# Expert layer: tokens fetched by indirect DMA a pair ahead, results added in place, weight rows dealt out in pairs, other places at the end

## The chip, the cores and the metric

One NeuronCore of a Trainium2 chip runs the whole program; seven cores are idle. The metric is the time of one execution on the device, in microseconds (us). Below, PE is the matrix engine (PEld its weight loads), DVE, ACT and POOL are the vector, scalar and GpSimd engines, and SP is the engine whose queue issues most of the DMAs.

## The reference

512 tokens of 1024 features go through two blocks. The first is a gated linear recurrence beside an attention, then a mixture of 16 experts in which each expert chooses its own 64 tokens; the second is another attention block with a feed-forward part, which the change does not touch. The expert layer, cut to what matters:

```
def expert_choice_moe(h, w_router, w_gate, w_up, w_down):
    cap = EC_CAPACITY_FACTOR * length // N_EXPERTS            # 64
    aff = softmax(h @ w_router)                               # [512, 16]
    gate, idx = lax.top_k(swapaxes(aff, 1, 2), cap)           # per expert
    xe = h[bidx, idx]
    hid = silu(einsum("becd,edf->becf", xe, w_gate)) * einsum("becd,edf->becf", xe, w_up)
    ye = einsum("becf,efd->becd", hid, w_down) * gate[..., None]
    return zeros_like(h).at[bidx, idx].add(ye)
...
x = x + g2 * expert_choice_moe(rms_norm(x, norm2_g) * (1 + sc2) + sh2, ...)
```

All is float32. Each expert has three 1024x1024 matrices, 12 MiB; the 16 experts have 192 MiB, or 201.3 MB, and every byte of it is read once.

## The kernel before, in words

**Stages.** `first_mixer` and the merge end in `mix_out` (L937), which multiplies by w_out, adds the product to `X` (the tokens, 128 partitions x 4 x 1024, in SBUF), transposes X (L955) and forms the router's logits. `router` (L982) takes the softmax, and in eight rounds of max and match_replace the 64 tokens of each expert; its result `sl` says for each token and expert which of the 64 slots it holds. `moe` (L1024) is the expert layer. Then come the second block's stages, from L1197 on.

**The loop over pairs.** `moe` takes two experts at a time, p = 0 to 7, with 64 slots each, so 128 columns. For a pair, `prep` (L1100 on) compares `sl` with a row of numbers to make a one-hot matrix D (L1089), scales it by each token's 1/rms, and gathers the tokens by 32 matmuls of X with D (L1105, 64 instructions on PE, as float32 goes through twice); DVE and ACT apply sc2 and sh2 on the way out of PSUM (L1107, L1110) into `xe`, which is already transposed. Then G = xe·w_gate and U = xe·w_up (both `gemm`, L1083, 32 matmuls of 64 slots x 512 each, 64 instructions), `back` (L1116: D once more, four transposes into `oh`, L1119, and the gate's values by four matmuls, L1124), `prep` of the next pair, hy = silu(G)·U (L1148), eight transposes (L1150), the down product Y (L1083). Y is split into a high and a low part in `yh` (L1173 to L1175), and 16 matmuls with `oh` (L1178, L1179) put each slot's result at its token; DVE adds them to `ACC` (L1181, L1184), two tiles of their own. In the last pair POOL adds ACC to X (L1171) and the products go straight into X. `ye` is the name for Y times gate and g2; the profile shows it as `hy`, as the buffer is shared.

**The order.** Each engine runs its instructions in the order in which a scheduler has put them, which stands before the run. It lets the scatter and the gather of the next pair run between the matmuls of a gemm.

**The weights.** Each weight load is 1 MiB: of 128x2x1024 (two rows of 4 KB per partition, 128 rows apart), issued by SP in the order of use. `mload` (L1035) deals out places for them in a fixed order, `kinds`: six "x1", three "raw", three "hl" (each two halves of 512 KB, L1052), three "x2", with four single places more and the two of ACC in the first round, 21 MiB in all, loaded before the layer starts. A load waits on SP until the matmuls on the former content of its place are done, and all loads behind it on SP wait with it. The last pair's down product goes by `gemm_parts` (L1062), in three parts of 512, 256 and 256 columns; its 12 loads (rows of 2 KB and 1 KB) use the three "x2" places and `rw2`, in turn, three times (L1046, L1059).

Of the kernel before, what the change touches and what calls it, by code (L numbers as in the profile page):

```python
# [20 lines left out]
def constants():  # L21
# [31 lines left out]
    iota = np.repeat(np.arange(1, 65, dtype=f)[None, :], 128, axis=0)  # L53
    return {
# [6 lines left out]
    }  # L61

# [6 lines left out]
class Build:  # L69
# [111 lines left out]
    def first_mixer(self):  # L181
# [19 lines left out]
        at = 0  # L201
# [12 lines left out]
        put("n2", I["norm2_g"][0].rearrange("(r p) -> r p", p=128), 8)  # L214
        put("lb", I["hg_lb_logits"].rearrange("a b (h p) -> (a b h) p", p=128), 16)
        put("hgn", I["hg_norm_g"][0].rearrange("(r p) -> r p", p=128), 4)
        self.prow = rows
# [9 lines left out]
        nc.vector.tensor_copy(self.pcol, tp[:, :128])  # L227
        cs = p1.tile([128, 8, 32], F32, name="cs")
# [157 lines left out]
        es1.close()  # L386
        esw = ExitStack()
# [20 lines left out]
    def ctx_part(self, cx, rest):  # L408
# [20 lines left out]
        def shift(i):  # L429
            for j, at in enumerate((0, 1, 2, 3)):  # L430
                if at == i:
                    self.mod_col(cx, pc, (self.sh2, self.sc2)[j // 2], 3 + j // 2, j % 2)
# [18 lines left out]
        nc.vector.scalar_tensor_tensor(self.sc2, self.sc2, 1.0, self.c("n2"), op0=ALU.add, op1=ALU.mult)  # L451
# [473 lines left out]
    def mod_col(self, pool, psp, out, wi, half, tag="mr"):  # L925

        nc = self.nc
        for s, row in self.mod_rows(pool, psp, wi, tag, (half,)):
# [4 lines left out]
            c = 8 * wi + 4 * s  # L933
            nc.vector.tensor_tensor(out[:, 4 * s:4 * s + 4], ps[:, :8].rearrange("p (k i) -> p k i", i=2)[:, :, 0],
                                    self.c("bmod")[:, c:c + 4], op=ALU.add)

    def mix_out(self, end):  # L937
# [3 lines left out]
        nc.sync.dma_start(wr, I["w_router"][0].rearrange("(k p) e -> p k e", p=128))  # L941
# [19 lines left out]
        for n, ks in enumerate(self.wN(I["w_out"][0], 0, 1024)):  # L961
            s = slice(n * 256, (n + 1) * 256)
            for b in range(4):
# [18 lines left out]
    def router(self):  # L982

        nc, mo, ms, pp = self.nc, self.mo, self.ms, self.pmx
        iota = self.iota = ms.tile([128, 64], F32, name="iota")
        nc.sync.dma_start(iota, self.I["k_iota"])
        rs = self.rs = ms.tile([128, 4], F32, name="rs")
# [3 lines left out]
        e = self.aff = ms.tile([128, 4, 16], F32, name="aff")  # L991
# [32 lines left out]
    def moe(self):  # L1024
# [4 lines left out]
        acc = [(self.mwx2, "acc0"), (self.mwx2, "acc1")]  # L1029
        kinds = ["x1"] * 6 + ["raw"] * self.nraw + ["hl"] * (self.nhl // 2) + ["x2"] * 3  # L1030
        self.tail = False
        todo = (kinds[:6] + [(self.rw1, "rw2"), (self.rw2, "rw")] + kinds[6:] +
                [(self.rw1, "rw"), (self.rw2, "rw2")] + acc)

        def mload(src, last):  # L1035
            if last == 2 and not self.tail:

                self.tail = True
                todo[:] = ["x2", "x2", "x2", (self.rw2, "rw2")] * 3
            if not todo:  # L1040
                todo.extend(k for k in kinds if not last or k != "hl")
            kind = todo.pop(0)
            shape = [128, src.shape[1], src.shape[2]]
# [10 lines left out]
            if kind == "raw":  # L1054
                t = self.wload(src, [128, 2, 1024])
            else:
                pool, n = (self.mwx, 6) if kind == "x1" else (ms, 3)
                t = pool.tile(shape, F32, name="mwt", tag="mwt", bufs=n)
                nc.sync.dma_start(t, src)  # L1059
            return [t[:, i] for i in range(shape[1])]  # L1060

        def gemm_parts(ps, lhs, wa, wb):  # L1062

            ws = [w.rearrange("(k p) f -> p k f", p=128) for w in (wa, wb)]
            for y, c in zip(ps, parts):
                for kk in range(2):
                    tl = [mload(w[:, 4 * kk:4 * kk + 4, c], 2) for w in ws]
# [19 lines left out]
        def onehot(p, tag, prev=None):  # L1087
            D = ms.tile([128, 4, 128], F32, name="D", tag=tag, bufs=1)
            ins = nc.vector.tensor_tensor(D.rearrange("p b (a s) -> p b a s", a=2),  # L1089
                                          self.iota.unsqueeze(1).unsqueeze(1).to_broadcast([128, 4, 2, 64]),  # L1090
                                          self.sl[:, :, 2 * p:2 * p + 2].unsqueeze(3).to_broadcast([128, 4, 2, 64]),
                                          op=ALU.is_equal)
            if prev:
                self.after(ins, prev)
            return D

        def prep(p):

            Ds = onehot(p, "Ds")
            nc.vector.tensor_tensor(Ds, Ds, self.rs.unsqueeze(2).to_broadcast([128, 4, 128]), op=ALU.mult)  # L1100
            xe = XE[p % 2]
            for k in range(8):
                ps = self.psmm()[:, :128]
                for b in range(4):
                    nc.tensor.matmul(ps, self.X[:, b, k * 128:(k + 1) * 128], Ds[:, b], start=(b == 0), stop=(b == 3))  # L1105
                if k % 2:
                    nc.scalar.activation(xe[:, k], ps, AF.Identity, bias=self.sh2[:, k:k + 1],  # L1107
                                         scale=self.sc2[:, k:k + 1])
                else:
                    ins = nc.vector.tensor_scalar(xe[:, k], ps, self.sc2[:, k:k + 1], self.sh2[:, k:k + 1],  # L1110
                                                  op0=ALU.mult, op1=ALU.add)
            return xe, ins

        def back(p, prev):

            D = onehot(p, "D", prev)  # L1116
# [3 lines left out]
            oh = ms.tile([128, 512], F32R, name="oh", tag="oh", bufs=1)  # L1120
            nc.scalar.activation(oh, ps, AF.Copy)
            gps = self.psmm()
            for b in range(4):
                nc.tensor.matmul(gps[:, :16], D[:, b], self.aff[:, b], start=(b == 0), stop=(b == 3))  # L1124
            gc = ms.tile([128, 1], F32, name="gc", tag="gc", bufs=2)
            for a in range(2):
                nc.vector.tensor_copy(gc[64 * a:64 * a + 64], gps[64 * a:64 * a + 64, 2 * p + a:2 * p + a + 1])
            return oh, gc
# [3 lines left out]
        xe, ins = prep(0)  # L1132
        for p in range(8):
# [11 lines left out]
            oh, gc = back(p, ins)  # L1145
            if p < 7:
                xe, ins = prep(p + 1)
            nc.vector.tensor_tensor(hs, hs, U, op=ALU.mult)  # L1148
            for k in range(8):
                nc.tensor.transpose(tp[:, k], hs[:, k * 128:(k + 1) * 128], self.ident)  # L1150
# [14 lines left out]
            yh = self.rw1.tile([128, 2, 1024], F32R, name="yh", tag="rw")  # L1165
            if p == 0:
                ACC = [pl.tile([128, 2, 1024], F32, name="acc", tag=t) for pl, t in acc]
                ACC = [ACC[b // 2][:, b % 2] for b in range(4)]
            elif p == 7:
                for b in range(4):  # L1170
                    nc.gpsimd.tensor_tensor(self.X[:, b], self.X[:, b], ACC[b], op=ALU.add)  # L1171
# [516 lines left out]
```

## Time and profile before

| | |
|---|---|
| median of 3 runs (lowest to highest) | 1816.25 us (1812.9 to 1819.8) |
| the profiled execution, its own time | 1816.96 us |
| its span in the trace | 1815.2 us |
| PE busy | 1710.9 us, 94% |
| DVE, ACT, POOL busy | 45%, 36%, 7% |
| moved by DMA | 327.73 MB, 181 GB/s over the span |
| first gate matmul of the expert layer | 641.7 us |
| first matmul of the second block (L1197) | 1142.8 us |
| chain that ended last | PE 63% of the span, DMA 1% |

The shares of the span are means over stages with different limits. The span is cut into 40 slices on the page, of 45.4 us each: the expert layer fills those from 642 to 1143 us, and from 726 to 1089 us, eight slices in a row, the DMA engines are nine tenths busy and more, which they are in hardly any other slice. PE's line shows nine tenths nearly everywhere. A PE row of the timeline is a run of instructions on one line that were not interrupted, its time in us, and in brackets how long PE stood idle before it and what ended that.

### The profile page before, as it was taken

To read this page: it belongs to the slowest core of one execution; us is meant where nothing else is said; L and a number is where in the kernel's file an instruction comes from. 1 tells how busy PE (TensorE), PEld (TensorE's weight loads), DVE (VectorE), ACT (ScalarE), POOL (GpSimd) and SP (SyncE) were. 2 spreads that over 40 slices of the span, in tenths; PEclk is the share of its full clock that TensorE was granted. 3 is DMA by queue.
4 is the path that set the end of the run, shared out by engine and by line. 5 is a ranking of instruction groups with operands and counts; after the bars stand their busy time and mean duration, and the time that the engine had idled before them with its cause. 6 is when DMAs were issued, how large, how long until landed. Compare 5 with 4: busy or idle time off the path is not lost.

```text
span 1815.2 us, 26611 instructions
## 1 busy us (share of the span) xinstructions
PE 1710.9 (94%) x11031; PEld 1247.3 (69%) x11031; DVE 824.7 (45%) x1605; ACT 655.2 (36%) x1137; POOL 131.9 (7%) x153
## 2 busy tenths in 40 slices
PE   5999899999999599999999998899999999999999
PEld 3987679666669553444434433697677989898989
DVE  5536885855343511221221221656675543434342
ACT  4638984656432210010000000655563242323131
POOL 0100000122110000000000010410221000000000
PEclk9999999999999799999999999999999999999999
DMA  9562122112458578999999996451002222323231
GB/s 308 184 206 76 48 71 65 60 37 92 168 174 298 210 304 317 409 409 384 393 375 362 407 383 229 131 163 50 22 24 70 83 91 84 115 72 116 71 115 48
DMA packets 177393, 327.73 MB, mean 181 GB/s; under 512 B 8580, under 2 KB 115816, under 8 KB 177272
## 3 DMA queue, kind: packets, MB, share of 16 engines
q1 hardware_dynamic: 176480, 325.44, 49.9%
q8 instruction: 87, 1.43, 0.3%
q10 hardware_dynamic: 744, 0.51, 0.1%
q14 instruction: 34, 0.28, 0.0%
q0 software_dynamic: 48, 0.08, 0.0%
HBM read 323.91 MB, written 2.10 MB: 180 GB/s over the span
## 4 chain that ended last, share of the span: by engine, by line
PE 63%; DVE 4%; DMA 1%; ACT 1%; issue 1%; POOL 0%; SPq 0%; DVEq 0%; ACTq 0%
PE mm L90 10%; PE mm L89 10%; PE mm L91 10%; PE G L1083 7%; PE U L1083 6%; PE Y L1083 5%; PE mm L1105 3%; PE po L1615 1%; PE mm L1178 1%; PE pt L1568 1%; PE mm L1179 1%; PE sc L1547 1%; DMA wraw<-in_w_in_dram 1%; PE sc L1548 1%; PE Y L1071 0%
## 5 line engine op out<-in xcount | busy, mean ns | idle before, releaser
L81 ACT ACTIVATE whi<-wraw 128x1024 fp32r<-128x1024 f32 (+1 forms) x171 | 173.4, 1018 | 365.0 <-PE mm L89 178.2
L83 DVE TENSOR_TENSOR wlo<-wraw,whi 128x1024 fp32r<-128x1024 f32 (+1 forms) x171 | 207.9, 1218 | 110.4 <-ACT whi L81 109.5
L90 PE MATMUL mm<-whi,ul 128*128 128x256 f32 x512 | 144.3, 282 | 0.0
L91 PE MATMUL mm<-whi,uh 128*128 128x256 f32 x512 | 143.2, 281 | 0.0
L89 PE MATMUL mm<-wlo,uh 128*128 128x256 f32 x512 | 143.1, 281 | 0.0
L90 PE MATMUL mm<-HXh,wlo 128*128 128x512 f32 x256 | 102.2, 399 | 1.8 <-DVE wlo L83 1.8
L89 PE MATMUL mm<-HXl,whi 128*128 128x512 f32 x256 | 103.5, 404 | 0.0
L91 PE MATMUL mm<-HXh,whi 128*128 128x512 f32 x256 | 101.2, 395 | 0.0
L89 PE MATMUL mm<-H,whi 128*128 128x512 f32 x256 | 99.7, 390 | 0.0
L91 PE MATMUL mm<-H,whi 128*128 128x512 f32 x256 | 99.6, 389 | 0.0
L90 PE MATMUL mm<-H,wlo 128*128 128x512 f32 x256 | 99.6, 389 | 0.0
L90 PEld LDWEIGHTS mm<-whi,ul 128*128 128x128 f32 x512 | 96.5, 188 | 1.0 <-DVE ul L1651 0.8
L89 PEld LDWEIGHTS mm<-wlo,uh 128*128 128x128 f32 x512 | 96.2, 188 | 0.2
L91 PEld LDWEIGHTS mm<-whi,uh 128*128 128x128 f32 x512 | 96.2, 188 | 0.0
L1105 PEld LDWEIGHTS mm<-D,X 128*128 128x128 f32 x512 | 61.9, 199 | 18.5 <-issue 15.4
L1660 DVE SCALAR_TENSOR_TENSOR X<-mm,r,X 128x256 f32<-128x256 f32 x64 | 30.9, 483 | 88.2 <-PE mm L91 88.2
L1105 PE MATMUL mm<-D,X 128*128 128x128 f32 x512 | 66.7, 288 | 2.8 <-DVE D L1100 1.8
L1148 DVE TENSOR_TENSOR hy<-hy,U 128x1024 f32<-128x1024 f32 x8 | 9.8, 1222 | 124.4 <-PE U L1083 124.4
L1083 PE MATMUL Y<-mwt,xh 128*64 128x512 f32 x240 | 59.9, 594 | 5.4 <-DVE xh L1151 5.4
L1646 DVE TENSOR_SCALAR r<-mm 128x512 f32<-128x512 f32 x32 | 22.1, 692 | 85.2 <-PE mm L91 85.2
L1173 DVE SCALAR_TENSOR_TENSOR hy<-Y,gc,g 128x512 f32<-128x512 f32 (+1 forms) x17 | 11.6, 715 | 106.4 <-PE Y L1083 100.2
L90 PEld LDWEIGHTS mm<-HXh,wlo 128*128 128x128 f32 x256 | 48.4, 189 | 13.8 <-DVE wlo L83 2.6
(539 smaller groups left out, 4073.0 us busy)
## 6 DMA issues: line engine op xcount, KB each, us to landing
mwt<-in_w_exp_gate_dram SPq DMA_DIRECT2D x41, 1024.0 KB, 9.1
mwt<-in_w_exp_up_dram SPq DMA_DIRECT2D x35, 1024.0 KB, 10.6
mwt<-in_w_exp_down_dram SPq DMA_DIRECT2D x33, 1024.0 KB, 13.2
wraw<-in_w_in_dram SPq DMA_DIRECT2D x29, 1024.0 KB, 5.1
wraw<-in_w_mod_dram SPq DMA_DIRECT2D x16, 1024.0 KB, 6.9
wraw<-in_w_up_dram SPq DMA_DIRECT2D x16, 1024.0 KB, 5.6
wraw<-in_w_down_dram SPq DMA_DIRECT2D x16, 1024.0 KB, 5.1
mwh<-in_w_exp_up_dram SPq DMA_DIRECT2D x30, 512.0 KB, 9.2
```

Of the source, the lines that this page charges most:

```text
L81: i1 = self.nc.scalar.activation(hi, src, AF.Copy)
L83: i2 = self.nc.vector.tensor_tensor(lo, src, hi, op=ALU.subtract)
L89: mm(ps, ah, bl, start=first, stop=False)
L90: mm(ps, al, bh, start=False, stop=False)
L91: mm(ps, ah, bh, start=False, stop=last)
L1083: nc.tensor.matmul(ps[64 * a:64 * a + 64, n], lhs[:, k, 64 * a:64 * a + 64], tl[a][k2][:, n * 512:(n + 1) * 512], start=(k == 0), stop=(k ...
L1105: nc.tensor.matmul(ps, self.X[:, b, k * 128:(k + 1) * 128], Ds[:, b], start=(b == 0), stop=(b == 3))
L1178: nc.tensor.matmul(ps, oh[:, b * 128:(b + 1) * 128], yh[:, 1, s], start=True, stop=False)
L1179: nc.tensor.matmul(ps, oh[:, b * 128:(b + 1) * 128], yh[:, 0, s], start=False, stop=True)
L1547: nc.tensor.matmul(sc, QS[:, h, s], KDl[:, br, p // 2, :n], start=True, stop=False)
L1646: nc.vector.tensor_scalar(r, ps, 0.0, None, op0=ALU.max)
L1660: nc.vector.scalar_tensor_tensor(self.X[:, b, s], ps, r2[:, b:b + 1], self.X[:, b, s], op0=ALU.mult, op1=ALU.add)
```

## The change

`mix_out` writes X to a DRAM copy `XD` (four DMAs from POOL's queue). A new function `chosen(p)` makes D and multiplies it by a table of 18 columns, which gives the gate, the token's number and its 1/rms for each slot; POOL then starts an indirect DMA that reads the 128 tokens' rows (4 KB each, 512 KB) from XD into `xg`. `prep` scales `xg` and transposes it (eight transposes). `chosen` of a pair is called a pair ahead. The scatter of two pairs (0 and 1, 2 and 3, 4 and 5) is summed in PSUM and added to X in place; pairs 6 and 7 go alone; ACC is gone. Weight rows 2p and 2p+1 of a block of 256 go to one partition, so that a partition's two rows are one piece of 8 KB in memory; every operand that meets them by its rows (`chunk(k)`: the transposes of X, xg and hy, sc2, sh2, the router's weights) is taken with a stride of two. The halves "hl" stay rows of 4 KB. Place "x3" is new and ACC's two places are gone, so 20 MiB are loaded before the layer starts. The last pair's 12 places are now x1, x1, rw2, x2, x2, x2, x1 (four times), rw2, x2.

```diff
+def chunk(k):
+    return slice(k // 2 * 256 + k % 2, k // 2 * 256 + 256, 2)
...
+        self.XD = dp.tile([512, 1024], F32, name="XD")
...
             for k in range(4):
-                nc.tensor.matmul(ps[:, 2 * k:2 * k + 2], row[:, k * 128:(k + 1) * 128], self.selc,
+                at = k // 2 * 256 + k % 2
+                nc.tensor.matmul(ps[:, 2 * k:2 * k + 2], row[:, at:at + 256 - k % 2:2], self.selc,
                                  start=True, stop=True)
...
-                    nc.tensor.transpose(tp[:, b * 128:(b + 1) * 128], self.X[:, b, k * 128:(k + 1) * 128], self.ident)
+                    nc.tensor.transpose(tp[:, b * 128:(b + 1) * 128], self.X[:, b, chunk(k)], self.ident)
...
+                if b == 3:
+                    nc.gpsimd.dma_start(self.XD.rearrange("(b p) f -> p b f", p=128)[:, :, s], self.X[:, :, s])
...
+        nc.gpsimd.tensor_copy(self.aff[:, :, 16], iota[:, 64:])
+        nc.gpsimd.tensor_copy(self.aff[:, :, 17], rs)
...
-        kinds = ["x1"] * 6 + ["raw"] * self.nraw + ["hl"] * (self.nhl // 2) + ["x2"] * 3
+        kinds = ["x1"] * 6 + ["raw"] * self.nraw + ["hl"] * (self.nhl // 2) + ["x2"] * 3 + ["x3"]
...
-                [(self.rw1, "rw"), (self.rw2, "rw2")] + acc)
+                [(self.rw1, "rw"), (self.rw2, "rw2")])
...
-                todo[:] = ["x2", "x2", "x2", (self.rw2, "rw2")] * 3
+                todo[:] = ["x1", "x1", (self.rw2, "rw2"), "x2", "x2", "x2", "x1", "x1", "x1", "x1",
+                           (self.rw2, "rw2"), "x2"]
...
-            wa = wa.rearrange("(k p) f -> p k f", p=128)
-            wb = wb.rearrange("(k p) f -> p k f", p=128)
+            ws = [w.rearrange("(k p j) f -> p k j f", p=128, j=2) for w in (wa, wb)]
             for kk in range(4):
-                tl = [mload(w[:, 2 * kk:2 * kk + 2, :], last) for w in (wa, wb)]
+                tl = [mload(w[:, kk], last) for w in ws]
...
+        def chosen(p):
+            if p > 7:
+                return None
+            xg = self.mwx2.tile([128, 1024], F32, name="xg", tag="xg", bufs=1)
+            D = onehot(p, "D")
+            ps = self.psmm()[:, :18]
+            for b in range(4):
+                nc.tensor.matmul(ps, D[:, b], self.aff[:, b], start=(b == 0), stop=(b == 3))
+            g = ms.tile([128, 18], F32, name="gs", tag="gs", bufs=3)
+            nc.vector.tensor_copy(g, ps)
+            at = ms.tile([128, 1], U32, name="at", tag="at", bufs=2)
+            nc.vector.tensor_copy(at, g[:, 16:17])
+            nc.gpsimd.indirect_dma_start(xg, None, self.XD, bass.IndirectOffsetOnAxis(ap=at, axis=0))
+            return xg, g
+        def prep(p, xg, g):
+            nc.vector.tensor_scalar(xg, xg, g[:, 17:18], None, op0=ALU.mult)
             xe = XE[p % 2]
-            for k in range(8):
-                ps = self.psmm()[:, :128]
-                for b in range(4):
-                    nc.tensor.matmul(ps, self.X[:, b, k * 128:(k + 1) * 128], Ds[:, b], start=(b == 0), stop=(b == 3))
...
+            for k0 in range(0, 8, 4):
+                ps = self.psmm()
+                for k in range(k0, k0 + 4):
+                    nc.tensor.transpose(ps[:, (k - k0) * 128:(k - k0 + 1) * 128], xg[:, chunk(k)], self.ident)
...
-            oh, gc = back(p, ins)
+            oh = back(p)
...
             if p < 7:
-                xe, ins = prep(p + 1)
+                xe = prep(p + 1, *ch)
+                gs, ch = ch[1], chosen(p + 2)
...
-            if p == 0:
-                ACC = [pl.tile([128, 2, 1024], F32, name="acc", tag=t) for pl, t in acc]
-                ACC = [ACC[b // 2][:, b % 2] for b in range(4)]
-            elif p == 7:
-                for b in range(4):
-                    nc.gpsimd.tensor_tensor(self.X[:, b], self.X[:, b], ACC[b], op=ALU.add)
+            yh = (ms if p % 2 else self.rw1).tile([128, 2, 1024], F32R, name="yh", tag="rw")
+            held.append((oh, yh))
...
+                if p in (0, 2, 4):
+                    continue
                 for b in range(4):
...
+                    parts_ = [(o, y[:, i, s]) for o, y in held for i in (1, 0)]
+                    for i, (o, v) in enumerate(parts_):
+                        nc.tensor.matmul(ps, o[:, b * 128:(b + 1) * 128], v, start=(i == 0), stop=(i == len(parts_) - 1))
+                    nc.vector.tensor_tensor(self.X[:, b, s], ps, self.X[:, b, s], op=ALU.add)
```

Left out are the setup's new small tile (b_mod and norm2_g in rows of 256, three DMAs on ACT's queue and two transposes), a place for rows of the last pair, and renamed variables.

**How the order moves.** On PE, pair 0, from the end of U to the start of Y (U and Y are the up and down products, `xe` the gathered tokens, `hy` silu(G)·U). Before:

```order
L1083 MATMUL U<-mwt,xe 64x512 x8
L1119 MATMUL mm<-ca,D 128x128 x4
L1124 MATMUL mm<-aff,D 128x16 x4
L1105 MATMUL mm<-D,X 128x128 x32
L1150 MATMUL tp<-ca,hy 128x128 x8
```

Now:

```order
L1120 MATMUL U<-mwt,xe 64x512 x8
L1171 MATMUL mm<-ca,D 128x128 x4
L1155 MATMUL mm<-ca,xg 128x128 x8
L1204 MATMUL tp<-ca,hy 128x128 x8
L1140 MATMUL mm<-aff,D 128x18 x4
L1120 MATMUL Y<-mwt,xh 64x512 x8
```

The 32 gathering matmuls are eight transposes now, and the four small matmuls of `chosen`, for pair 2, stand behind the transposes of hy.

On PE, pair 2 of the changed kernel, from its gate product G on (L1232 is the scatter of pairs 0 and 1, L1171 the transposes for `oh`):

```order
L1232 MATMUL mm<-yh,oh 128x512 x28
L1120 MATMUL G<-mwt,xe 64x512 x16
L1171 MATMUL mm<-ca,D 128x128 x4
L1155 MATMUL mm<-ca,xg 128x128 x4
L1120 MATMUL G<-mwt,xe 64x512 x7
L1155 MATMUL mm<-ca,xg 128x128 x4
L1140 MATMUL mm<-aff,D 128x18
L1120 MATMUL G<-mwt,xe 64x512
L1140 MATMUL mm<-aff,D 128x18 x3
L1171 MATMUL mm<-ca,D 128x128 x4
L1120 MATMUL G<-mwt,xe 64x512 x7
L1120 MATMUL U<-mwt,xe 64x512
```

Behind these stand the next `L1155` transposes, eight of them, for pair 4: nine matmuls of a gemm lie between the last of the L1140 rows, whose gather they need, and them. The scheduler has pulled the preparation of pairs 3 and 4 into pair 2's gate product; pair 4 has the same form for pairs 5 and 6.

On SP, the loads of the last pair's down product. Before:

```order
L1059 DMA mwt<-in_w_exp_down_dram 128x4x512 x2
L1046 DMA mwo<-in_w_exp_down_dram 128x4x512
L1059 DMA mwt<-in_w_exp_down_dram 128x4x512
L1232 DMA gk<-in_g_k_dram 128x192
L1233 DMA gk<-in_g_q_dram 128x64
L1237 DMA al<-in_k_alibi_dram 128x512
L1059 DMA mwt<-in_w_exp_down_dram 128x4x256 x2
```

Now:

```order
L1096 DMA mwt<-in_w_exp_up_dram 128x2048 x8
L1078 DMA mwt<-in_w_exp_down_dram 128x2x512 x8
L1078 DMA mwt<-in_w_exp_down_dram 128x2x256 x16
L1283 DMA gk<-in_g_k_dram 128x192
L1284 DMA gk<-in_g_q_dram 128x64
L1288 DMA al<-in_k_alibi_dram 128x512
```

All of the last pair's loads now stand ahead of the second block's small loads, and a full load reads as 128x2048, one row of 8 KB per partition.

## Rows read from the trace of the kernel before

**Rows 1.** The page: busy time of the engines, and DMA packets
```profile
PE 1710.9 (94%) x11031; PEld 1247.3 (69%) x11031; DVE 824.7 (45%) x1605; ACT 655.2 (36%) x1137; POOL 131.9 (7%) x153
...
DMA packets 177393, 327.73 MB, mean 181 GB/s; under 512 B 8580, under 2 KB 115816, under 8 KB 177272
```
**Rows 2.** Windows: us, busy time per engine, clock, DMA share, GB/s
```profile
core 0: us, PE busy (x) PEld busy (x) DVE busy (x) ACT busy (x) POOL busy (x), PEclk, DMA share, GB/s
20.00:30.00 10.00, 9.83 (x80) 5.04 (x78) 6.96 (x13) 0.77 (x2) 0.00 (x0) 1.00 1.07 338
560.00:565.00 5.00, 5.00 (x39) 4.52 (x38) 3.22 (x6) 2.52 (x4) 0.00 (x0) 1.00 1.03 410
620.00:645.00 25.00, 13.93 (x84) 11.65 (x86) 13.88 (x28) 3.11 (x5) 0.00 (x0) 0.65 0.24 86
645.40:1137.00 491.60, 464.78 (x2274) 200.82 (x2270) 103.46 (x178) 40.98 (x69) 9.71 (x13) 1.00 0.95 368
700.00:820.00 120.00, 115.17 (x586) 51.92 (x586) 28.61 (x49) 10.56 (x18) 0.00 (x0) 1.00 1.01 401
...
1100.00:1112.00 12.00, 12.00 (x58) 3.93 (x54) 0.00 (x0) 0.00 (x0) 0.00 (x0) 1.00 0.06 21
```
**Rows 3.** Waits of SP's queue, 645 to 1140 us: total, times, longest
```profile
SPq L1059 <- PE G L1083: 103.3, 35, 15.1
SPq L1059 <- PE Y L1083: 69.3, 16, 12.9
SPq L1059 <- PE U L1083: 57.4, 27, 16.8
```
**Rows 4.** Timeline of SP's queue: start, us, DMA issues
```profile
645.39 3.80 SPq L1059 DMA_DIRECT2D mwt<-in_w_exp_down_dram  x3
...
1112.54 0.37 SPq L1059 DMA_DIRECT2D mwt<-in_w_exp_down_dram  x1
...
1131.55 0.47 SPq L1046 DMA_DIRECT2D mwo<-in_w_exp_down_dram  x1
```
**Rows 5.** Timeline of PE: start, us, instructions, idle before
```profile
631.64 10.14 PE L1105 MATMUL mm<-D,X 128*128 128x128 f32 x64 [1.77 <-DVE D L1100]
641.72 10.52 PE L1083 MATMUL G<-mwt,xe 128*64 128x512 f32 x48
...
670.68 7.41 PE L1105 MATMUL mm<-D,X 128*128 128x128 f32 x64
677.92 1.04 PE L1150 MATMUL tp<-ca,hy 128*128 128x128 f32 x8
...
834.83 1.07 PE L1083 MATMUL G<-mwt,xh 128*64 128x512 f32 x2
...
838.26 3.65 PE L1083 MATMUL G<-mwt,xh 128*64 128x512 f32 x14
...
1137.31 0.43 PE L1071 MATMUL Y<-mwo,xh 128*64 128x256 f32 x1
...
1142.78 0.60 PE L1197 MATMUL tp<-ca,X 128*128 128x128 f32 x4
```
**Rows 6.** Waits of PE, 645 to 1140 us: total, times, longest
```profile
PE mm L1178 <- DVE yh L1175: 7.9, 6, 1.5
...
PE Y L1071 <- DMA mwt<-in_w_exp_down_dram: 1.3, 2, 0.8
```
**Rows 7.** DMA issues, whole run: times, KB each, median us to landing
```profile
mwt<-in_w_exp_down_dram SPq DMA_DIRECT2D x33, 1024.0 KB, 13.2
...
levf<-in_k_lev_dram POOLq DMA_DIRECT2D x1, 80.0 KB, 5.0
```
**Rows 8.** Line L265, DVE: ns min/median/max, first and last start
```profile
L265 DVE TENSOR_SCALAR X<-X,rs x4: 748/748/753, 17.9 to 19.9; 128x1024 f32<-128x1024 f32 x4
```
**Rows 9.** Lines L955, L1470, weight loads: ns min/median/max
```profile
L955 PEld LDWEIGHTS tp<-ca,X x32: 138/140/143, 569.3 to 607.9; 128*128 128x128 f32 x32
...
L1470 PEld LDWEIGHTS hp<-wraw,Xc x64: 184/199/226, 1191.8 to 1211.6; 128*64 128x64 f32 x64
```

More of the change, by code (lines that the diff above doesn't have):

```diff
@@ L227, in first_mixer @@
         nc.vector.tensor_copy(self.pcol, tp[:, :128])
+        tp = pst.tile([128, 512], F32, name="tp", tag="tr", bufs=2)
+        for j in range(2):
+            nc.tensor.transpose(tp[:, 12 * j:12 * j + 12], r256[:, j::2], self.ident[:12, :12])
+        self.pair = p1.tile([128, 2, 12], F32, name="pair")
+        nc.vector.tensor_copy(self.pair, tp[:, :24].rearrange("p (j r) -> p j r", j=2))
         cs = p1.tile([128, 8, 32], F32, name="cs")
@@ L386, in first_mixer @@
         es1.close()
+        dp = self.es.enter_context(tc.tile_pool(name="xd", bufs=1, space=bass.MemoryType.DRAM))
+        self.XD = dp.tile([512, 1024], F32, name="XD")
         esw = ExitStack()
@@ L450, in ctx_part @@
         shift(3)
-        nc.vector.scalar_tensor_tensor(self.sc2, self.sc2, 1.0, self.c("n2"), op0=ALU.add, op1=ALU.mult)
+        pairs = lambda t: t.rearrange("p (k j) -> p k j", j=2)
+        nc.vector.scalar_tensor_tensor(pairs(self.sc2), pairs(self.sc2), 1.0, self.pair[:, :, 8:]
+                                       .rearrange("p j k -> p k j"), op0=ALU.add, op1=ALU.mult)
         nc.scalar.activation(KY, FR, AF.Sigmoid, scale=-1.0)
@@ L923, in mod_bc, with mod_col @@
         return end
-    def mod_col(self, pool, psp, out, wi, half, tag="mr"):
+    def mod_col(self, pool, psp, out, which, half, tag="mr"):
         nc = self.nc
-        for s, row in self.mod_rows(pool, psp, wi, tag, (half,)):
+        for s, row in self.mod_rows(pool, psp, 3 + which, tag, (half,)):
             ps = psp.tile([128, 512], F32, name="mr", tag=tag, bufs=self.nmr)
             for k in range(4):
-                nc.tensor.matmul(ps[:, 2 * k:2 * k + 2], row[:, k * 128:(k + 1) * 128], self.selc,
+                at = k // 2 * 256 + k % 2
+                nc.tensor.matmul(ps[:, 2 * k:2 * k + 2], row[:, at:at + 256 - k % 2:2], self.selc,
                                  start=True, stop=True)
-            c = 8 * wi + 4 * s
-            nc.vector.tensor_tensor(out[:, 4 * s:4 * s + 4], ps[:, :8].rearrange("p (k i) -> p k i", i=2)[:, :, 0],
-                                    self.c("bmod")[:, c:c + 4], op=ALU.add)
+            r = 4 * which + 2 * s
+            nc.vector.tensor_tensor(out[:, 4 * s:4 * s + 4].rearrange("p (k j) -> p k j", j=2),
+                                    ps[:, :8].rearrange("p (k j i) -> p k j i", j=2, i=2)[:, :, :, 0],
+                                    self.pair[:, :, r:r + 2].rearrange("p j k -> p k j"), op=ALU.add)
     def mix_out(self, end):
@@ L1042, in mload @@
             kind = todo.pop(0)
+            if len(src.shape) == 4:
+                pool, tag, n = kind + (None,) if isinstance(kind, tuple) else place[kind]
+                t = pool.tile([128, src.shape[1] * 2, src.shape[3]], F32, name="mwt", tag=tag, bufs=n)
+                for i in range(src.shape[1]):
+                    nc.sync.dma_start(t[:, 2 * i:2 * i + 2], src[:, i])
+                return [t[:, i] for i in range(t.shape[1])]
             shape = [128, src.shape[1], src.shape[2]]
@@ L1056, in mload @@
             else:
-                pool, n = (self.mwx, 6) if kind == "x1" else (ms, 3)
-                t = pool.tile(shape, F32, name="mwt", tag="mwt", bufs=n)
+                pool, tag, n = place[kind]
+                t = pool.tile(shape, F32, name="mwt", tag=tag, bufs=n)
                 nc.sync.dma_start(t, src)
@@ L1117, in back @@
+        def back(p):
+            D = onehot(p, "D")
             ps = self.psmm()
@@ L1119, in back @@
                 nc.tensor.transpose(ps[:, b * 128:(b + 1) * 128], D[:, b], self.ident)
-            oh = ms.tile([128, 512], F32R, name="oh", tag="oh", bufs=1)
+            oh = ms.tile([128, 512], F32R, name="oh", tag="oh", bufs=2)
             nc.scalar.activation(oh, ps, AF.Copy)
-            gps = self.psmm()
-            for b in range(4):
[L1124 to L1128, printed above, removed]
+            return oh
         wg, wu, wd = I["w_exp_gate"][0], I["w_exp_up"][0], I["w_exp_down"][0]
         XE = {0: self.xp.tile([128, 8, 128], F32, name="xe", tag="g1")}
-        xe, ins = prep(0)
+        ch = chosen(0)
+        xe = prep(0, *ch)
+        gs, ch = ch[1], chosen(1)
+        held = []
         for p in range(8):
```

72 lines of the change are left out of this document (35 added, 37 removed).

## The prediction, made before the result was known

> **What bounds the kernel now.** I began with the page: PE is busy for 94% of the span [rows 1], and the share alone says "PE bound". But the change lies in the expert layer, where 192 MiB of weights must come in, so I read that stage's windows [rows 2]. From the first reload (645.4 us) to the end of the loads (1137 us) the DMA engines moved 368 GB/s at a share of 0.95. Steady stretches reach 410 GB/s with rows of 4 KB; rows of 1 KB, at the program's start, gave 338 at a share of 1.07, so there too the engines were full. What the stage loses against 410: the 171 MiB (179.3 MB) loaded in it need 438 us at 409.5 GB/s and took 491.6. About 3 us of the difference are shorter rows in the last pair, so some 51 us went into idle or half idle engines, most plainly from 1100 to 1112 us, at 21 GB/s.
>
> Who kept them idle: the waits of SP's queue [rows 3] name G, U and Y, 230 us together. A load stands at the head of the queue until PE has finished with its place. The other way round PE hardly waits: 1.3 us for the last pair's down weights [rows 6]. So in this stage **PE sets the pace and DMA is close behind it**: a pair takes PE (1142.8 - 641.7) / 8 = 62.6 us [rows 5], and its 24 MiB take DMA 61.5 us at 409.5 GB/s. Whatever is taken from PE counts only until DMA becomes the bound, a microsecond per pair later; beyond that only what DMA gains counts. The end of the stage to watch is the first transpose of the second block, at 1142.78 us [rows 5]. What stands behind it is unchanged: 1816.96 - 1142.78 = 674.2 us, taken from the profiled execution (1816.96 us), which lies 0.7 us above the median of the runs.
>
> **The start of the stage.** Before, the 64 gathering instructions run from 631.64 us for 10.1 us, at a clock that was partly granted at half (mean 0.65 in that window) [rows 2, 5], and G begins at 641.72. Now: four small matmuls (1 us), copy, cast and issue (1 us), the gather, scaling (0.75 us, as the row of the same shape on L265 [rows 8]), eight transposes (1.04 us [rows 5], 2.1 at half clock), one eviction (0.4). The nearest row for the gather is the only other DMA on POOL's queue, 5.0 us for 80 KB [rows 7]; 432 KB more at 410 GB/s is 1.1 us. That gives 643.0 us. Bounds: 641 (a gather as short as 4 us) and 650, if it lasts as long as a loaded queue's weight load (13.2 us [rows 7]). I take 644.7, 3 us late: nearer the lower bound, as the row of the same queue is, with room for a kind of transfer that no row shows. Before, the first place came free 3.7 us after G began [rows 4, 5]; so the first reload starts at 648.4.
>
> **PE's side.** Seven gathers inside the loop go, 7 x 7.41 = 51.9 us; seven times eight transposes come, 7 x 1.04 = 7.3 us [rows 5]. Scatters of two pairs together: three of the six waits for the split, 1.3 us each, go, 4 us [rows 6]; the scatter matmuls themselves stay as many. Cut gemms: by the two orders a gemm runs in 68 pieces before and 40 now. Two pieces of 2 and 14 instructions took 1.07 and 3.65 us [rows 5], that is 0.215 us per instruction and 0.64 us per piece; 28 pieces fewer are worth 0 (if the ends are only modelled) to 18 us, and I take 16, as the gap to the next piece's start agrees. Against it stand two new waits. In pairs 2 and 4 the transposes for the pair after next stand only nine gemm matmuls (4 us) behind the small matmuls that start their gather; everything behind them on PE waits too, G and U of that pair included. A gather chain of 7.4 us leaves 3.4 us each, one of 13.2 us 10; I take 10 for both together. Weight loads of transposes taken with a stride: 199 against 140 ns [rows 9], 0 to 7 us over 120 of them, and I take 0, as a load overlaps the matmul before it. Sum: 644.7 + 501.1 - 51.9 + 7.3 - 4 - 16 + 10 = **1091 us**, between 1080 and 1115.
>
> **DMA's side.** 20 MiB instead of 21 wait ready, so 172 MiB follow the first reload. A packet's price from the two steady windows, per engine (1/16 of 338 and of 409.5 GB/s): 48.5 ns for 1 KB, 160 ns for 4 KB, so 11.3 ns and 0.0363 ns per byte [rows 2]; a row of 8 KB then moves at 424 GB/s, one of 2 KB at 382. No row shows 8 KB, so the bounds are 409.5 (nothing gained) and 440 (the slope alone); I take 424, on the line through both. 134 MiB at 424: 331.4 us. 30 MiB of halves, still 4 KB, at 409.5: 76.8. The last 8 MiB, 4 of 2 KB and 4 of 1 KB rows: 11.0 + 12.4. Seven gathers of 512 KB: 9.0. Sum 440.6 us, the last load lands at 1089.0. Its first user began 5.5 us ahead of the stage's end before [rows 5]; with the wait for the landing 6.5: **1095.5 us**. The new places of the last pair are what lets its loads run on: before, a load that stood at 1112.54 [rows 4] waited while DMA was idle.
>
> DMA ends 4 us behind PE, near enough that not all waits vanish; I add 4 us. The stage ends at 1099.5. Elsewhere: the 32 transposes in the output product, now strided, cost 0 to 2 us [rows 9], I take 1; the copy of X (2 MB, 5 us at 410) goes out while DMA is at 86 GB/s [rows 2] and the router's long DVE chain runs, so 0, or 5 us if the first gather had to wait for it; setup's small loads hide behind the first weights, 0. Total 674.2 + 1099.5 + 1 = **1775 us**, 42 us below the profiled execution.
>
> **Rivals.**
> 1. *Rows of 8 KB move no faster* (they may be split into the packets of before, under 8 KB each [rows 1]). For it: no packet of that size is seen on the weights' queue. Against: the step from 1 to 4 KB gave 21%. Then 134 MiB take 343.1 us, 11.7 more: 1786 us. Here a page bears on it: the Trainium skill, "DMA: Bandwidth & Descriptors", section "Why small descriptors are slow (HBM only)", gives a packet a fixed cost of about three cycles of 32 bytes, by which the step from 4 to 8 KB would be worth 1.1%, an estimate that makes it 1783 us. By that rule the step from 1 to 4 KB would be 7%; the trace shows 21%, so I don't follow it for the size.
> 2. *Places still come free in bursts.* The queue is in order, one place is fewer, and the stalls in pairs 2 and 4 hold back U's and Y's places for all that follows. If half of the 51 us stays, 21 us more than I allowed: 1796 us.
> 3. *Slow gathers.* At 20 us each, G begins at about 658 and the two stalls are 17 us each: PE ends at 658.6 + 501.1 - 51.9 + 7.3 - 4 - 16 + 34 = 1129, and the time is 1804 us; at 14 us it is about 1785. For it: 128 rows by address, on a queue that shares its engines with a full weight stream. Against: 5.0 us for the one transfer seen there.
> 4. *Slower than before.* The same gather from about 24 us on: each microsecond costs three (the start and two stalls), so at 24 us the gain is gone (1129 + 12 = 1141) and at 35 us the time is 1849. Only a gather three times the longest median load seen here would do it; nothing in the rows speaks for that, but no row shows an indirect transfer either.
>
> **How the numbers follow.** Forecast (8 KB rows help, DMA bounds) 0.42; rival 1 0.26; rival 2 0.13; rival 3 0.11; rival 4 0.05; a gain of under 0.5% by several of these together 0.03. A measurement of this kernel tells some 0.5% (9 us) from no change, so 1807 and below is faster. Rival 3 lies half beyond 1796 and its upper edge near that line: of its 0.11 I give 0.03 to "same". Faster 0.42 + 0.26 + 0.13 + 0.08 = 0.89, less 0.03 for what I have not seen, 0.86; same 0.08; slower 0.06. Range: downward, DMA at 440 GB/s saves 12 us more, but PE at 1080 to 1091 then bounds it, about 1757; upward it takes in rivals 1 and 2 and most of 3, 1802.
>
> **What would show it.** Right: DMA at over 410 GB/s from 650 to about 1090 us without the gap before the last pair; SP's waits for PE shrink to a fraction of 230 us and PE's waits for weights appear; packets fall by some 16,000 (151 MiB in half as many, 3,000 more for the copy and the gathers); gathers land within 6 to 10 us; PE stalls of 3 to 8 us ahead of the transposes of L1155 in pairs 2 and 4; the first transpose of the second block near 1100 us. Packets unchanged, or 410 GB/s at the most, is rival 1. DMA shares under 0.95 between 700 and 1050 us, with SP waiting for PE, is rival 2. Gathers of over 14 us, with PE idle at L1155, are rivals 3 and 4. The prediction is wrong in kind if PE is still never waiting for weights.

## The result, and the profile after

The changed kernel takes **1792.13 us** (median of 4 runs, 1786.53 to 1792.99) against 1816.62 (4 runs): ratio 0.9871, 95% interval 0.9853 to 0.989. It is faster, by 24 us where the forecast said 42; the time lies within the stated range, 17 us above the forecast. The profiled execution took 1792.71 us, its span 1790.9. The page, busy times and packets, answers to [rows 1]:

```profile
PE 1659.4 (93%) x10585; PEld 1208.1 (67%) x10585; DVE 809.0 (45%) x1598; ACT 655.0 (37%) x1137; POOL 135.3 (8%) x163
...
DMA packets 159430, 333.97 MB, mean 186 GB/s; under 512 B 8409, under 2 KB 115649, under 8 KB 139985
```

The packets fell by 18,000 (16,000 were forecast), and 19,445 of them (159430 - 139985) now have 8 KB or more, against 121 before: the paired rows do move as one packet. Windows of the stage, beside those of [rows 2] (us; busy time and instructions per engine; clock; DMA share; GB/s):

```profile
700.00:820.00 120.00, 102.11 (x452) 41.59 (x448) 24.36 (x47) 11.76 (x22) 3.34 (x3) 0.91 0.98 404
820.00:1000.00 180.00, 155.67 (x680) 61.26 (x680) 30.13 (x56) 14.57 (x24) 2.39 (x2) 0.94 0.99 405
800.00:820.00 20.00, 18.56 (x74) 6.72 (x74) 2.07 (x4) 0.79 (x2) 0.00 (x0) 0.83 0.83 331
920.00:940.00 20.00, 13.99 (x52) 5.13 (x50) 2.89 (x4) 1.51 (x3) 0.00 (x0) 0.74 0.78 300
```

DMA is nearly full, but not quite: in two stretches of 20 us it falls to 331 and 300 GB/s. And PE is less busy than before, 102 us of 120 against 115, at a granted clock of 0.91 and 0.94 instead of 1.00 and 0.99. SP's waits, beside [rows 3], and PE's, beside [rows 6] (total, times, longest):

```profile
SPq L1096 <- PE Y L1120: 58.2, 14, 13.5
SPq L1096 <- PE G L1120: 54.4, 19, 19.1
SPq L1096 <- PE U L1120: 27.3, 7, 12.1
```

```profile
PE mm L1155 <- DVE xg L1150: 20.0, 3, 6.8
PE tp L1204 <- DVE hy L1202: 16.9, 6, 6.1
PE mm L1232 <- DVE yh L1225: 9.8, 7, 2.2
```

On the line of the full loads SP's waits for PE shrank from 230 to 140 us (over all lines, of which [rows 3] shows only this one, from 366 to 197). But no wait of PE for weights is listed: PE still ends last. Instead it waits for the gathered rows (L1155; one of the three waits, of 6.8 us, is the first gather's, ahead of the stage), and for hy (L1204), which before cost 1.4 us a time and now as much as 6.1. Where that happens is in PE's timeline, pair 2 (start, us, instructions, idle before and its releaser; the last row is the first transpose of the second block, as in [rows 5]):

```profile
765.73 3.22 PE L1120 MATMUL G<-mwt,xe 128*64 128x512 f32 x13
...
776.02 1.95 PE L1155 MATMUL mm<-ca,xg 128*128 128x128 f32 x8 [6.64 <-DVE xg L1150]
...
789.95 4.45 PE L1120 MATMUL U<-mwh,xe 128*64 128x512 f32 x18
800.46 1.98 PE L1204 MATMUL tp<-ca,hy 128*128 128x128 f32 x8 [6.07 <-DVE hy L1202]
803.23 15.72 PE L1120 MATMUL Y<-mwt,xh 128*64 128x512 f32 x64 [0.79 <-DVE xh L1205]
...
1119.46 0.60 PE L1248 MATMUL tp<-ca,X 128*128 128x128 f32 x4
```

6.64 us ahead of the transposes of the gathered rows; 6.07 ahead of the transposes of hy. The second has another mechanism, which DVE's timeline of the same stretch shows:

```profile
788.12 0.15 DVE L1144 CAST at<-gs 128x1 uint32<-128x1 f32 x1
789.29 0.41 DVE L1162 TENSOR_SCALAR xe<-mm,sc,sh 128x128 f32<-128x128 f32 x1 [1.02 <-PE U L1120]
798.21 0.75 DVE L1150 TENSOR_SCALAR xg<-xg,gs 128x1024 f32<-128x1024 f32 x1 [8.51 <-DMA xg<-XD,at]
798.88 0.41 DVE L1162 TENSOR_SCALAR xe<-mm,sc,sh 128x128 f32<-128x128 f32 x1
799.20 1.21 DVE L1202 TENSOR_TENSOR hy<-hy,U 128x1024 f32<-128x1024 f32 x1
```

The token numbers of pair 5 are cast at 788.12 and its gather starts; DVE's queue then comes to the scaling of the rows that are not there yet (L1150) and stands 8.51 us, with hy (L1202), whose last input was ready when U ended at 794.40, queued behind it. PE waits for hy. The gathers took, from issue to landing (min, median, max over the eight):

```profile
DMA to landing us min/median/max: 4.2/9.1/9.2
```

4.2 us with idle queues (the first), 9.1 beside the weights. Pair 4 repeats all this 130 us later (waits of 6.50 and 5.23 us). In and behind each stall PE has a lower granted clock (a mean of 0.91 is a share of the stretch at 1.2 instead of 2.4 GHz): the 64 instructions of Y at 803.23 took 15.72 us, and 13.95 in the kernel before.

### The profile page after: what moved, and what is told of

The parts are those of the page before. It is cut to its first block, busy times and chain, and to the rows that moved or that the text cites. A ratio compares the mean times of both kernels' runs of the same rounds, so it can differ in the third digit from the quotient of the medians.

```text
span 1790.9 us, 25752 instructions
## 1 busy us (share of the span) xinstructions
PE 1659.4 (93%) x10585; PEld 1208.1 (67%) x10585; DVE 809.0 (45%) x1598; ACT 655.0 (37%) x1137; POOL 135.3 (8%) x163
## 2 busy tenths in 40 slices
DMA packets 159430, 333.97 MB, mean 186 GB/s; under 512 B 8409, under 2 KB 115649, under 8 KB 139985
## 4 chain that ended last, share of the span: by engine, by line
PE 79%; DVE 8%; ACT 5%; DMA 4%; issue 2%; POOL 1%; DVEq 0%; ACTq 0%; POOLq 0%
PE mm L97 15%; PE mm L96 14%; PE mm L98 14%; PE G L1120 6%; PE Y L1120 6%; PE U L1120 5%; DMA xg<-XD,at 2%; PE mm L1232 2%; PE po L862 2%; PE po L1666 1%; PE pt L854 1%; PE pt L1619 1%; DVE wlo L90 1%; PE Y L1108 1%; PE sc L1598 1%
## 5 line engine op out<-in xcount | busy, mean ns | idle before, releaser
L1202 DVE TENSOR_TENSOR hy<-hy,U 128x1024 f32<-128x1024 f32 x8 | 9.8, 1219 | 144.5 <-PE U L1120 122.1
L1120 PE MATMUL Y<-mwt,xh 128*64 128x512 f32 x288 | 69.2, 637 | 4.1 <-issue 2.5
L1120 PE MATMUL G<-mwt,xe 128*64 128x512 f32 x240 | 62.1, 612 | 0.0
L1120 PE MATMUL U<-mwt,xh 128*64 128x512 f32 x256 | 57.3, 592 | 0.0
L1224 ACT ACTIVATE yh<-hy 128x512 fp32r<-128x512 f32 (+1 forms) x17 | 10.3, 605 | 127.9 <-DVE hy L1223 127.7
```

The source lines that it names most:

```text
L1120: nc.tensor.matmul(ps[64 * a:64 * a + 64, n], lhs[:, k, 64 * a:64 * a + 64], tl[a][k2][:, n * 512:(n + 1) * 512], start=(k == 0), stop=(k ...
```

## The experiments

Theory A: the gain that is missing went into these stalls. Theory B: the weights' DMA sets the time, and a stall only moves a wait. The runs were made in groups, each on one chip together with the kernel before, and all ratios are to that kernel on the same chip; the changed kernel's is 0.9871, and 0.9883 (0.9863 to 0.9903) when it was run again in the last group.

**The scaling on POOL.**

```diff
-            nc.vector.tensor_scalar(xg, xg, g[:, 17:18], None, op0=ALU.mult)
+            nc.gpsimd.tensor_scalar(xg, xg, g[:, 17:18], None, op0=ALU.mult)
```

> The changed kernel with one line moved: the scaling of the gathered rows runs on POOL instead of DVE. Theory A (the missing gain went into stalls of PE in pairs 2 and 4: 6.6 and 6.5 us ahead of the transposes of the gathered rows, and 6.1 and 5.2 us ahead of the transposes of hy, because DVE stood 8.5 us at the scaling with hy queued behind it): the two waits for hy fall to the usual 1.4 us, the two waits ahead of the transposes grow by what POOL is slower, 1 to 2 us each, and the time falls by 4 to 9 us against the changed kernel's 1792. Theory B (the weights' DMA sets the time, a stall only moves waiting from one place to another): the stalls change likewise, the time stays within 3 us of 1792.

Measured: 0.9876 (0.9848 to 0.9904), no difference; a miss for A's number.

```profile
PE mm L1155 <- POOL xg L1150: 25.9, 3, 9.0
...
PE tp L1204 <- DVE hy L1202: 8.2, 6, 1.4
```

The waits for hy did fall, by 8.7 us, which shows that it was DVE's queue that held hy. But POOL takes 2.84 us for what DVE does in 0.75, and the other wait grew by 5.9. The sum changed by 3 us, too little to be seen in the time.

**The order pinned.** The scaling and the transposes of the next pair's rows stand behind the last matmul of this pair's U.

```diff
-            nc.vector.tensor_scalar(xg, xg, g[:, 17:18], None, op0=ALU.mult)
+            ins = nc.vector.tensor_scalar(xg, xg, g[:, 17:18], None, op0=ALU.mult)
+            if behind:
+                self.after(ins, behind)
...
-                    nc.tensor.transpose(ps[:, (k - k0) * 128:(k - k0 + 1) * 128], xg[:, chunk(k)], self.ident)
+                    ins = nc.tensor.transpose(ps[:, (k - k0) * 128:(k - k0 + 1) * 128], xg[:, chunk(k)], self.ident)
+                    if behind:
+                        self.after(ins, behind)
...
-                xe = prep(p + 1, *ch)
+                xe = prep(p + 1, *ch, last)
```

> The changed kernel with an order only: the scaling and the transposes of the gathered rows of the next pair must stand behind the last matmul of this pair's U, in every pair, as they do in pairs 0 and 1. The gather then has half a pair of time. Theory A: the four stalls (24 us, of which 3 us are usual) and the lower clock that follows them (granted 0.83 to 0.91 in the windows around them) go, PE no longer ends last, the DMA bound of the prediction takes over: 20 to 28 us less than 1792, some 1764 to 1772, and PE begins to wait for weights. Theory B: under 6 us less.

Run again beside the changed kernel:

> The changed kernel itself, beside the others on one chip: ratio to before within its interval of 0.985 to 0.989.

> The pinned kernel again, on the chip of the changed kernel: 8 to 14 us less than it, ratio to before 0.980 to 0.984.

Measured: 0.9817 (0.9797 to 0.9838), and beside the changed kernel on one chip 0.9798 (0.9775 to 0.9821) against 0.9883: 13 to 15 us less at medians of 1777.95 and 1790.92, or 10 by the ratios of the first runs, 0.9817 and 0.9871.

```profile
PE U L1120 <- DMA mwt<-in_w_exp_up_dram: 9.5, 9, 1.4
...
PE mm L1158 <- DVE xg L1151: 6.9, 1, 6.9
...
PE tp L1209 <- DVE hy L1207: 3.5, 8, 1.4
```

```profile
700.00:820.00 120.00, 115.39 (x528) 45.01 (x524) 23.09 (x43) 11.81 (x20) 1.89 (x2) 0.99 1.02 419
820.00:1000.00 180.00, 159.88 (x698) 62.75 (x698) 36.21 (x67) 15.28 (x27) 2.83 (x3) 0.98 1.02 419
```

This is the picture that the prediction had drawn for the change itself: one wait for gathered rows is left, the first, PE begins to wait for weights, the clock stays near 1.00, and DMA moves 419 GB/s without a gap. Direction and mechanism are A's; the size is less than A said. From the first G to the first transpose of the second block the traces have 501.1 us before, 479.4 in the changed kernel (478.2 when run again) and 461.5 here (462.9 when run again), so 15 to 18 us within the stage. Of these, 13 to 15 are PE's idle time, which was 50.7 us of the stage in the changed kernel and is 37.2 and 35.7 here.

**Each pair scattered alone.** Nothing is pinned.

```diff
-                if p in (0, 2, 4):
-                    continue
...
-            if p not in (0, 2, 4):
-                held = []
+            held = []
```

> The changed kernel with every pair scattered alone (16 matmuls and 8 additions into X per pair, as in pairs 6 and 7), nothing else. The order that comes out has the gather of pair p+2 start in the middle of pair p and its transposes a whole pair later; the doubled pull into pairs 2 and 4 is gone, without any order being pinned. Theory A (the stalls set the time, and it is the scatter of two pairs together that led the scheduler to them): as the pinned kernel, ratio to before 0.979 to 0.984, no wait of PE for gathered rows but the first, though there are more cuts of gemms (some 20 pieces more) and more waits for the split. Theory B (fewer scatters are themselves a gain): slower than the changed kernel, 0.988 or more.

Measured: 0.9801 (0.9777 to 0.9825), the same as the pinned kernel. In PE's waits only the first one for gathered rows is left:

```profile
PE tp L1204 <- DVE hy L1202: 8.3, 6, 1.4
PE mm L1155 <- DVE xg L1150: 7.0, 1, 7.0
```

So it is the scatter of two pairs together that, through the order the scheduler then chose, brought the stalls. Fewer scatters won nothing that the time shows: the split's waits were 9.6 us here, 9.8 in the changed kernel and 7.9 before [rows 6].

**Rows of 4 KB, in the changed and in the pinned kernel.**

```diff
 def chunk(k):
-    return slice(k // 2 * 256 + k % 2, k // 2 * 256 + 256, 2)
+    return slice(k * 128, k * 128 + 128)
...
-            ws = [w.rearrange("(k p j) f -> p k j f", p=128, j=2) for w in (wa, wb)]
+            ws = [w.rearrange("(k j p) f -> p k j f", p=128, j=2) for w in (wa, wb)]
```

> The changed kernel with the rows dealt out singly again (rows 128 apart, pieces of 4 KB, no strides in the transposes); gathers, scatter and places as in the changed kernel. Theory A (PE with its stalls sets the time): 0 to 6 us slower than 1792, as DMA has idle windows to fill. Theory B (DMA sets it): 10 to 13 us slower, 134 MiB at 409 instead of 424 GB/s. Both: DMA at 410 GB/s in the steady windows and about 17,000 packets more.

> The kernel with the pinned order, rows dealt out singly again (4 KB pieces). With the stalls gone DMA is full from the first reload to the last, so now the rate counts: 134 MiB at 409 instead of 419 GB/s, some 3.5 us, and 4 more by the prediction's 424; theory A: 4 to 12 us more than the pinned kernel (ratio to before 0.984 to 0.988 against its 0.9817), that is, rows of 8 KB are worth nothing where PE stalls and their full price where it does not. Theory B (rows of 8 KB never matter, as in the changed kernel): within 2 us of the pinned kernel.

Measured: changed kernel 0.987 (0.985 to 0.989), no difference. Pinned kernel 0.9842 (0.9819 to 0.9865), median 1784.22: slower than its 0.9798 and 0.9817 in both groups, by 4 to 8 us, though the intervals touch; beside the pinned kernel with the old places (below), on the same chip, 6 us (1778.03); inside the stage 472.2 us against 461.5 and 462.9. (The 3.5 us in the expectation is a slip: 134 MiB at 409 instead of 419 GB/s are 8 us, and with the 4 that are added there 12.) The windows of the changed and then of the pinned kernel with 4 KB rows:

```profile
700.00:820.00 120.00, 102.32 (x447) 41.43 (x443) 25.44 (x50) 12.83 (x23) 3.34 (x3) 0.91 1.02 405
820.00:1000.00 180.00, 158.59 (x697) 62.50 (x698) 31.74 (x58) 13.50 (x22) 2.39 (x2) 0.95 1.02 408
```

```profile
820.00:1000.00 180.00, 159.55 (x684) 62.40 (x682) 36.15 (x67) 14.26 (x26) 2.84 (x3) 0.95 1.03 409
```

409 GB/s with rows of 4 KB, 419 with 8 KB, both with full engines. PE's granted clock is lower as well in the pinned kernel with 4 KB rows (0.95 in this window against 0.98), and what that adds is not separated. In the changed kernel the slower rows just fill the time that the stalls leave (405 and 408 GB/s on the mean, where the 8 KB kernel reaches 404 and 405), so the faster rate is worth nothing there; without stalls it is worth something. The trace of the changed kernel with 4 KB rows even has a shorter stage, 474.2 us against 479.4 and 478.2: its gathers land in 7.8 us on the median instead of 9.1, and the waits for gathered rows and for hy are 33.3 us together instead of 36.9.

**The kernel before with the paired rows alone.** The setup, router, weights and chunks as in the change; the gather by matmuls, the scatter and the places as before.

```diff
-                    nc.tensor.matmul(ps, self.X[:, b, k * 128:(k + 1) * 128], Ds[:, b], start=(b == 0), stop=(b == 3))
+                    nc.tensor.matmul(ps, self.X[:, b, chunk(k)], Ds[:, b], start=(b == 0), stop=(b == 3))
```

> The kernel before with the paired rows alone (8 KB pieces and all strides that go with them); gather by matmuls, scatter and places as before. Theory A and the prediction: PE sets the pace there, so 0 to 4 us less than 1816, or up to 2 us more by the strided transposes. Theory B (DMA sets the time in both kernels): 10 to 13 us less.

Measured: 1.0037 (1.0022 to 1.0053), 7 us slower, which neither theory had. PE sets the pace there, so faster rows bring nothing, and the strides cost: the transposes of hy,

```profile
L1172 PEld LDWEIGHTS tp<-ca,hy x64: 194/209/219, 674.6 to 1117.5; 128*128 128x128 f32 x64
L1172 PE MATMUL tp<-ca,hy x64: 273/283/385, 674.7 to 1117.6; 128*128 128x128 f32 x64
```

load in 209 ns instead of 140 and take 283 instead of 273 (medians), and the 512 gathering instructions 281 instead of 275 ns; that is some 4 us of the 7. For the rest the traces have one thing to show: PE was granted half clock for 13.7 us of this stage and for 3.4 of the one before, worth some 5 us (an estimate, at half of PE's busy time there). Why the clock fell more often is open.

**The places at the end.** In the pinned kernel the old ones, in the kernel before the new ones.

```diff
-                todo[:] = ["x1", "x1", (self.rw2, "rw2"), "x2", "x2", "x2", "x1", "x1", "x1", "x1",
-                           (self.rw2, "rw2"), "x2"]
+                todo[:] = ["x2", "x2", "x2", (self.rw2, "rw2")] * 3
```

> The kernel with the pinned order, with the places of the kernel before for the last pair's down product (x2, x2, x2, rw2, three times over). If the places at the end carry what the prediction gave them, DMA stands idle again ahead of the last pair's down product, 10 us or more at under 50 GB/s, and the time is 6 to 12 us more than the pinned kernel's. If they are worth nothing (the tail is PE's), within 2 us of it.

> The kernel before with the new places for the last pair's down product alone. If they are worth what the prediction gave them, the idle DMA from 1100 to 1112 us is filled and the few waits of PE at the end go: 2 to 6 us less than before (0.997 to 0.999). If PE's own work sets the tail: within 2 us. The first run of this kind, in the pinned kernel, showed no difference.

Measured: 0.9805 (0.978 to 0.9829), as the pinned kernel; and 0.9985 (0.997 to 0.9999) for the kernel before, 0 to 5 us. DMA does thin out with the old places (pinned kernel):

```profile
1080.00:1090.00 10.00, 8.76 (x45) 3.52 (x41) 1.44 (x2) 0.63 (x1) 0.00 (x0) 1.00 0.65 208
```

208 GB/s, where the new places give 321. But PE is 8.8 us of these 10 busy, and behind the last load stands the same work of the last pair. The two runs do not tell a small gain from none.

**Every gather twice, in the changed and in the pinned kernel.**

```diff
             nc.gpsimd.indirect_dma_start(xg, None, self.XD, bass.IndirectOffsetOnAxis(ap=at, axis=0))
+            nc.gpsimd.indirect_dma_start(xg, None, self.XD, bass.IndirectOffsetOnAxis(ap=at, axis=0))
```

> The changed kernel with every gather issued twice into the same tile, one behind the other: from issue to the second landing some 18 us instead of 9. Theory A (a gather's time is on PE's path twice in pair 2 and twice in pair 4, and once at the start): five times 6 to 9 us, less what DMA has in hand meanwhile, 25 to 40 us more than the changed kernel (ratio to before 1.000 to 1.010). Theory B (only the bytes count): eight times 512 KB at 410 GB/s, 10 us more (ratio 0.993).

> The kernel with the pinned order and every gather issued twice. There a gather has about half a pair, 25 us and more, before PE needs it. Theory A: no new wait of PE for gathered rows but the one at the start (7 us becomes 16); the 3.5 MiB more take 9 us of a full DMA; 10 to 16 us more than the pinned kernel, a third to a half of what doubling costs the changed kernel. Theory B: the same surcharge in both kernels, within 4 us.

Measured: changed kernel 1.0098 (1.0073 to 1.0123), median 1832.38, about 41 us more than without; pinned kernel 0.9879 (0.9856 to 0.9902), 11 to 15 us more. PE's waits in the first:

```profile
PE mm L1156 <- DVE xg L1151: 35.2, 3, 11.9
PE tp L1205 <- DVE hy L1203: 31.2, 6, 12.9
```

29.5 us more waiting in these two groups than in the changed kernel, and 41 us more time. 5 of the 29.5 us are the first gather's. In the traces the stage grew from 479.4 to 512.3 us, 29 us of it as idle time of PE. Where a gather has 26 us and more to land in, as in the pinned kernel, the same extra transfers cost 11 to 15 us: 5 at the start, and some 9 for 3.5 MiB on a full DMA (an estimate, at 419 GB/s). This decides for A.

## Why the prediction was right and where it failed

**The bound.** "PE sets the pace and DMA is close behind it" held for the kernel before, where faster rows alone won nothing; that DMA would be the bound afterwards held only once the stalls were gone. The rest of the program went as forecast (1792.71 - 1119.46 = 673.3 us behind the stage, 674.2 taken).

**Its own signs.** Packets, the gathers' time to land and the stalls at L1155 came as listed. DMA at over 410 GB/s without a gap, waits of PE for weights and the first transpose near 1100 us (1119.5) did not, and the last sentence, "wrong in kind if PE is still never waiting for weights", is what the changed kernel shows. So the direction was earned, by the gathers that left PE (its busy time in the stage fell from 473.7 to 428.7 us). That the time lies in the range is owed to the range, drawn wide enough to take in rivals 1 and 2, and to that extent luck: the sum behind the forecast describes the pinned kernel, not this one.

**The start.** G began at 640.1 us (644.7 forecast, a little ahead of the lower bound, 641): the first gather took 4.2 us, less than the one row of POOL's queue had. PE was still at half clock (0.50 until 646.4 us), so the first place came free later, and the first reload started at 647.9. That this is near the 648.4 of the forecast is luck, two errors that cancel.

**DMA's side.** Right but for a size, and seen only where DMA was the bound, in the pinned kernel: rows of 8 KB move at 419 GB/s, not 424, a gain of 2.4% where the line through two windows gave 3.5%. The rule of the Trainium skill, "DMA: Bandwidth & Descriptors", section "Why small descriptors are slow (HBM only)", would have given 1.1%; the measured step lies between. In the pinned kernel the loads after the first ones are issued from 642.4 to 1083.8 us; with some 2 us for the last to land, an estimate, that is 443 us, against the forecast sum of 440.6. Rival 1 (rows of 8 KB no faster) is refuted by the rate; in time it came true for the changed kernel, where nothing was waiting for the faster rows.

**PE's side is the step that failed**: "I take 10 for both together". The sum said 446.5 us from G to the end of PE's chain; it was 479.4. What the runs showed in its place, by size:

- Four waits, not two. The transposes in pairs 2 and 4 were named (13.1 us together); that DVE would stand at the scaling with hy queued behind it was not, as the prediction never asked what stands behind the scaling in DVE's order (10 us more than before). From the cast to the landed rows a loaded chain took 10 us (788.12 to 798.21 in DVE's timeline above), in the middle of the bounds of 7.4 and 13.2, so the chain's length was not what was missed. (At 13.2 us, 9.2 would be left each, not 10.)
- The clock, on which the prediction put no price. It comes in stretches at 0.50: 50.5 us of the stage, with PE busy for 36.4 of them, where the kernel before had 3.4 us. Four of the stretches lie in and behind the four stalls (second group of rows below), with PE busy for 20.5 us; one is the start of G, 6.3 us, and three of 3.4 us stand elsewhere. Y of pair 2 shows what this costs: 3.6 us of it ran at half clock, and it took 1.8 us longer than before. Half of the busy time, 18 us, less 1.6 before, makes 17 us, an estimate, and 10 of them are the stalls'.
- The scatter: "three of the six waits for the split go, 4 us" did not happen (9.8 us, 7.9 before); later groups wait longer.

The stage from the first G to the first transpose of the second block, before, changed and pinned, and the four stretches of the changed kernel:

```profile
641.72:1142.78 501.06, 473.67 (x2329) 206.13 (x2329) 108.41 (x187) 44.89 (x75) 10.79 (x14) 1.00 0.94 365
640.09:1119.46 479.37, 428.66 (x1929) 172.16 (x1929) 94.02 (x176) 44.66 (x76) 9.07 (x16) 0.95 0.97 391
636.50:1097.95 461.45, 424.29 (x1929) 167.41 (x1929) 93.01 (x176) 43.59 (x76) 8.06 (x16) 0.99 1.00 406
```

```profile
772.70:779.50 6.80, 3.48 (x12) 2.11 (x14) 0.75 (x1) 0.00 (x0) 0.00 (x0) 0.50 1.01 420
796.60:806.80 10.20, 5.55 (x18) 2.69 (x20) 2.89 (x4) 1.06 (x2) 0.00 (x0) 0.50 0.93 375
902.40:909.20 6.80, 4.58 (x16) 2.43 (x18) 0.75 (x1) 0.00 (x0) 0.00 (x0) 0.50 1.03 427
926.30:936.50 10.20, 6.94 (x20) 3.06 (x22) 2.89 (x4) 1.05 (x2) 0.00 (x0) 0.50 0.78 300
```

PE was idle for 27.4 us of the stage before and for 50.7 after the change; the prediction's terms leave 33.4 (27.4 - 4 + 10). PE was busy for 428.7 us, and the terms leave 413.1 (473.7 - 51.9 + 7.3 - 16). So 17 us are missing in idle time and 16 in busy time, 33 in all. The waits above are 13 + 6 = 19 us against the first, the clock's 17 against the second; by this the term for the cut gemms held, as far as the modelled ends of matmuls let it be said.

**The places at the end** "are what lets its loads run on": they do, and it is worth 0 to 5 us.

**The rivals.** Rival 2 gave 1796 us, near the time, and its sign (DMA under full with SP waiting for PE) was seen at 800 and 920 us; its reason, half of it: the stalls held the places, the order of the queue by itself did not, as the pinned kernel shows with the same queue. Rivals 3 and 4 had the right mechanism and too low a price: three us per microsecond of gather were taken, and a second gather of about 8 us cost 41, five per microsecond (the start and four stalls; the bytes of the second gather are in it too). With gathers of 17 us the change was a loss; rival 4 put that point at 24, which is not three times the longest median load of 13.2 us, as its last sentence has it, but not quite twice.

**A version that beats both** is the pinned one, or the one that scatters each pair alone: 0.980 to 0.982 of the time before.

## What to carry to other kernels

When a transfer is issued "a pair ahead" in the program, look in the order that comes out at how far ahead it really is on each engine, and at what is queued behind its first reader on that reader's own engine: the second wait here was not on the engine that needed the data. A stall of PE costs more than its length (here some 10 us of lower clock came with 24 us of stalls), so take the clock behind it from rows after an idle stretch. And price a faster transfer at nothing until the profile shows someone waiting for it.

## What was not expected of the hardware

An indirect gather of 128 rows of 4 KB takes 4.2 us on idle queues, less than the 5.0 us of a plain 80 KB transfer on the same queue [rows 7], and 9.1 beside a full weight stream. Transposes that read every second column load in 209 ns instead of 140 [rows 9] and still lengthen each matmul by only 10 ns.
